# Sixteen low-half products of the first attention are made by GpSimd in place of VectorE

## The chip, the cores and the metric

The kernel runs on one core of one Trainium2 chip. The metric is the device time of one execution in microseconds (us), from the first to the last instruction and the little around them. Before the change three runs took 1171.39, 1173.42 and 1175.44 us; their median is 1173.42 us.

The core has five instruction queues. PE (TensorE) multiplies matrices, ACT (ScalarE) applies functions and scales, DVE (VectorE) and POOL (GpSimd) do elementwise work, SP (SyncE) starts transfers. Each queue is worked off in the order in which its instructions stand, and queues wait for each other by semaphores.

## The reference

The program is a two-layer encoder on 512 tokens of width 1024, in float32. Layer 0 is the even one. Its attention has two groups of eight heads that share one output projection. Group A is grouped-query attention with rotary positions. Group B (the diff's word for it is kind B) is latent attention, in which 32 of the 96 query and key columns carry the rotary part:

```
h = x
for layer in range(DEPTH):
    hn = rmsnorm(h, norm_mix[layer])
    if layer % 2 == 0:   h = h + hybrid_attention(hn, ...)      # A heads, B heads, concatenate, @ w_out
    else:                h = h + neighbourhood_attention(hn, ...)
    h = h + sq_relu_mlp(rmsnorm(h, norm_ffn[layer]), ...)

rope_1d: [x1*cos - x2*sin, x2*cos + x1*sin]
hybrid:  mixed = concatenate([oa, ob]);  return mixed @ w_out
```

The change touches the hybrid attention of layer 0 alone, which in the profile lies between about 68 and 264 us.

## The kernel before

**Two halves of a number.** The products must keep nearly float32 precision on a multiplier that takes rounded numbers. Every operand is therefore split: a high half, which ACT writes by a copy into the rounded type, and a low half, the number minus its high half, which costs one two-input subtraction on DVE or POOL. A product is three matmuls: high by high, high by low, low by high (`mm3`, lines 545, 546 and 547). `split` (line 899) makes the two halves of an activation: ACT at line 906, the low half at line 903. `chunk` (lines 206 to 250) makes those of weights: the high half at line 236, or at 246 where heads are regrouped, the low half at line 226. A weight chunk that is given an engine uses that engine for its low half; without one it is DVE's.

**The attention.** `attend` (line 1036) goes through the 16 heads, four blocks of 128 queries each. For each block PE makes the scores (line 1070, tile `s`), DVE scales them and takes the minimum (line 1074), ACT makes the exponentials (line 1076), DVE the reciprocal of the sum (line 1077), POOL scales by it (line 1078, in the tile `shared`). Some blocks later PE transposes the result (line 1045, tile `t`), ACT and DVE split it (lines 1047 and 1048), and PE multiplies with the values (line 1058, tile `o`). There are five score buffers in `shared`, two banks for `s`, two for `t`, one for `o`, three `mm` for the work in between.

**The work in between.** While heads run, PE is also given the projections of the B heads (`projB`, whose rotary part goes through `rope`), and, from the 36th block on, the output projection of the first four head pairs (`out_proj`). `fold` adds the halves of a finished head (line 1022) and, after the second head of a pair, splits the pair; the pairs are the operands of the output projection. The last four pairs are projected after the last head.

**Rotary positions.** `rope` makes a shuffled copy on DVE (line 603), a product with the cosines on POOL (line 605), a product with the sines on DVE (line 606) and the sum on DVE (line 609). In group A the shuffles of later tiles are transfers (`far`), the sine product is POOL's, and the sum is made at line 674 and split at lines 676 and 677.

**What sets the order.** In this part of the program a scheduler places the instructions on PE, ACT, DVE and POOL at build time, from its own estimates of what each costs. A change of engine for one instruction therefore reorders others. On the chip each queue keeps that order. POOL's queue also starts the transfers of line 832, which add sums of later weights in memory.

Of the kernel before, what the change touches and what calls it, by code (L numbers as in the profile page):

```python
# [12 lines left out]
ALU = mybir.AluOpType  # L13
# [5 lines left out]
P = 128  # L19
# [16 lines left out]
def encoder_kernel(ctx: ExitStack, tc: tile.TileContext, ins, out, dbg=None):  # L36
# [555 lines left out]
    sw16 = [q ^ 16 for q in range(32)]  # L592
    sw8 = [q ^ 8 for q in range(32)]

    def rope(src, cos, sin, mask, n=P, far=False):

        sh = scratch()
        if far:
            q = mask[0]
            for b in range(0, n, q):  # L600
                SP.dma_start(sh[b : b + q, :], src[b ^ q : (b ^ q) + q, :])
        else:
            DVE.stream_shuffle(sh[0:n, :], src[0:n, :], mask)
        c = scratch()
        POOL.tensor_tensor(c[0:n, :], src[0:n, :], cos[0:n, :], op=ALU.mult)
        (POOL if far else DVE).tensor_tensor(sh[0:n, :], sh[0:n, :], sin[0:n, :], op=ALU.mult)
        if far:
            return c, sh
        DVE.tensor_tensor(c[0:n, :], c[0:n, :], sh[0:n, :], op=ALU.add)
        return c  # L610
# [287 lines left out]

    w_uq, w_ukv = ins["ev_b_w_uq"][0], ins["ev_b_w_ukv"][0]

    def split(src, dst, then=lambda: None):
        def low():
            DVE.tensor_tensor(dst[:, 1, :], src, f32(dst[:, 0, :]), op=ALU.subtract)  # L903
            then()

        ACT.activation(dst[:, 0, :], src, AF.Copy)
        soon(low)
# [3 lines left out]
    def projB(g, last):  # L911
# [5 lines left out]
        def q_part():  # L917
            CQ = [s_.pair() for s_ in cqS]
            banks = three(3)
            for m in (2, 0, 1):  # L920
                for k in range(3):
                    hi, lo = (z[:, k % 2, m * P : (m + 1) * P] for z in weights(iq[k // 2]))
                    mm3(banks[m], hi, lo, CQ[k][:, 0, :], CQ[k][:, 1, :], k == 0, k == 2)
                    yield MM3
                if m == 2:
                    qc = scratch()
                    ACT.activation(qc, banks[2], AF.Copy)
                    qr = rope(qc, cosB, sinB, sw8)
                    stg = Slot()
                    split(qr, stg.pair())  # L930
                else:

                    Q.extend(Slot() for _ in range(2))
                    qa, qb = Q[2 * m].pair(), Q[2 * m + 1].pair()
                    split(banks[m], qa)
                    SP.dma_start(f32(qb[0:64, :, :]), f32(qa[64:128, :, :]))
                    for e, q in enumerate((qa, qb)):
                        j = 2 * m + e
                        SP.dma_start(f32(q[64:96, :, :]), f32(stg.pair()[32 * j : 32 * j + 32, :, :]))
            stg.free()  # L940
            if last:
                for s_ in cqS:
                    s_.free()
# [53 lines left out]

    w_out = ins["ev_w_out"][0]

    def out_proj(w, k0, ok, cols, name):  # L1000

        def ev(j, b):
            m = cols[j]
            DVE.tensor_tensor(hT[:, m, :], hT[:, m, :], b, op=ALU.add)
        gen = product(w, k0, ok, [(P * m, P) for m in cols], ev, three if name else None)
        if name:
            return name, gen
        for _ in gen:
            pass
# [4 lines left out]
    def fold(o, e):  # L1014
# [6 lines left out]
        def add():  # L1021
            DVE.tensor_tensor(pair[a : a + 64, :], o[0:64, :], c[0:64, :], op=ALU.add)
            if e:
                O.append(Slot())
                soon_a(lambda o=O[-1]: split(pair, o.pair()))

        soon(add)

# [122 lines left out]
    def step(h, i):  # L1151
        n = count[0]
        count[0] += 1
        if n == 35:

            ok = [s_.pair() for s_ in O]
            assert len(ok) == 4
            fill.add(*out_proj(w_out, 0, ok, [0, 1, 2], "out"))
            projB(1, True)
            fill.add(*out_proj(w_out, 0, ok, [3, 4, 5], "out"))  # L1160
            fill.add(*out_proj(w_out, 0, ok, [6, 7], "out"))
        if n == 22:
            beat.update(every=4.2, work=ahead0.steps())
        fill.run(1.5)
# [841 lines left out]
```

## Time and profile before

| what | value |
|---|---|
| median of three runs | 1173.42 us |
| the profiled execution's own time | 1173.18 us |
| its span, first to last instruction | 1171.4 us |
| PE busy over the span | 1144.9 us, 98% |
| DVE busy | 919.4 us, 78% |
| ACT busy | 668.2 us, 57% |
| POOL busy | 463.6 us, 40% |
| granted TensorE clock | 0.998 |

About 1.8 us of the profiled execution lie outside its span. The profiler takes one execution, and the times of single instructions are from it. A row of the timeline gives the start in us, the duration in us, the engine, the line, the operation, output and inputs, and in brackets the idle time ahead of it with what ended it. Matmuls overlap: one of 512 columns is shown with about 0.39 us, while the next starts 0.23 us later, so that a wait on PE is read from the distance of the starts rather than from the busy time.

### The profile page before, as it was taken

Reading aid. Unit: us, or ns where it says so; the run is one execution under the profiler, and the core shown is the slowest. Engines: PE = TensorE matmul, PEld = TensorE weight load, DVE = VectorE, ACT = ScalarE, POOL = GpSimd, SP = SyncE. Lnnn points to the kernel's source line nnn. Section 1 sums busy time; section 2 is a strip of 40 time slices with the busy share of each in tenths; the row PEclk is TensorE's granted clock in tenths of the full one; section 3 lists DMA queues with packets and bytes.
Section 4 is the critical chain, followed back from the end, with each engine's and each line's share of the span. In section 5 each row is a group of like instructions: output and inputs, shape, how many; then the busy total and the mean of one; then the engine's idle time right before and its main releaser. Section 6 shows DMA issues by size and latency. Waiting matters only on the chain.

```text
span 1171.4 us, 20855 instructions
## 1 busy us (share of the span) xinstructions
PE 1144.9 (98%) x7596; PEld 1029.6 (88%) x7596; DVE 919.4 (78%) x1617; ACT 668.2 (57%) x1147; POOL 463.6 (40%) x486
## 2 busy tenths in 40 slices
PE   9989999999999999999999999999999999999996
PEld 8667778888799999999988998988788999999995
DVE  5788988778978787998474676767896878799845
ACT  5468576664536656756253555645552665675625
POOL 3267253333668795000002243333185898600000
PEclk9999999999999999999999999999999999999999
DMA  7123467664577666768426497778566666765702
GB/s 273 55 79 84 122 147 202 176 143 129 114 172 196 162 149 198 234 215 278 131 82 163 131 247 190 191 189 209 178 128 183 170 166 158 193 208 174 249 2 72
DMA packets 129543, 191.55 MB, mean 164 GB/s; under 512 B 12659, under 2 KB 81184, under 8 KB 128736
## 3 DMA queue, kind: packets, MB, share of 16 engines
q1 hardware_dynamic: 112304, 136.61, 37.1%
q0 software_dynamic: 14976, 29.38, 15.5%
q10 hardware_dynamic: 2160, 24.22, 6.2%
q8 instruction: 60, 0.98, 0.4%
q14 instruction: 43, 0.35, 0.1%
HBM read 167.75 MB, written 52.43 MB: 188 GB/s over the span
## 4 chain that ended last, share of the span: by engine, by line
PE 79%; DVE 10%; DMA 4%; ACT 3%; issue 2%; POOL 1%; SPq 0%; DVEq 0%; POOLq 0%; ACTq 0%
PE mm L547 7%; PE mm L545 7%; PE mm L546 7%; PE t L1444 3%; PE t L1443 2%; PE t L1445 2%; PE mm L418 2%; PE mm L416 2%; PE mm L417 2%; PE s L1070 2%; PE o L1058 2%; PE mm L1445 2%; PE mm L1443 2%; PE mm L1444 2%; PE t L1045 2%
## 5 line engine op out<-in xcount | busy, mean ns | idle before, releaser
L545 PE MATMUL mm<-a,whi 128*128 128x512 f32 x407 | 164.8, 407 | 0.3 <-ACT whi L236 0.2
L547 PE MATMUL mm<-a,wlo 128*128 128x512 f32 x407 | 160.2, 395 | 1.6 <-DVE wlo L226 1.5
L546 PE MATMUL mm<-a,whi 128*128 128x512 f32 x407 | 160.9, 395 | 0.1
L337 DVE TENSOR_TENSOR wlo<-raw,whi 128x896 fp32r<-128x896 f32 x80 | 110.5, 1388 | 28.6 <-ACT whi L336 28.4
L236 ACT ACTIVATE whi<-raw 128x1024 fp32r<-128x1024 f32 (+3 forms) x86 | 80.4, 939 | 86.4 <-PE s L546 29.7
L226 DVE TENSOR_TENSOR wlo<-raw,whi 128x1024 fp32r<-128x1024 f32 (+4 forms) x83 | 99.2, 1197 | 36.1 <-ACT whi L236 34.4
L336 ACT ACTIVATE whi<-raw 128x896 fp32r<-128x896 f32 x80 | 75.4, 949 | 83.6 <-PE o L546 22.9
L547 PEld LDWEIGHTS mm<-a,wlo 128*128 128x128 f32 x407 | 76.4, 188 | 19.4 <-DVE wlo L226 3.0
L545 PEld LDWEIGHTS mm<-a,whi 128*128 128x128 f32 x407 | 76.5, 188 | 16.1 <-ACT whi L236 1.3
L546 PEld LDWEIGHTS mm<-a,whi 128*128 128x128 f32 x407 | 76.8, 189 | 14.1 <-DVE a L903 0.4
L1609 POOL DMA_DIRECT2D a<-a x16 | 8.7, 545 | 185.7 <-PE mm L546 169.2
L1078 POOL TENSOR_SCALAR shared<-shared,ti 128x512 f32<-128x512 f32 x64 | 48.3, 758 | 84.5 <-DVE ti L1077 53.5
L418 PE MATMUL mm<-a,wlo 128*128 128x256 f32 x280 | 78.8, 282 | 0.7 <-DVE wlo L337 0.7
L417 PE MATMUL mm<-a,whi 128*128 128x256 f32 x280 | 78.5, 280 | 0.0
L416 PE MATMUL mm<-a,whi 128*128 128x256 f32 x280 | 78.4, 280 | 0.0
L1444 PE MATMUL t<-a,whi 128*128 128x256 f32 x264 | 74.2, 281 | 0.6 <-DVE a L1389 0.5
L1443 PE MATMUL t<-a,whi 128*128 128x256 f32 x264 | 73.9, 280 | 0.0
L1445 PE MATMUL t<-a,wlo 128*128 128x256 f32 x264 | 73.9, 280 | 0.0
L1701 POOL TENSOR_SCALAR shared<-shared,ti 128x256 f32<-128x256 f32 x64 | 35.5, 566 | 95.9 <-DVE ti L1700 83.6
L330 POOL TENSOR_TENSOR raw<-raw 128x512 f32<-128x512 f32 x40 | 67.8, 1695 | 3.1
L1341 DVE TENSOR_TENSOR wlo<-a,whi 128x1024 fp32r<-128x1024 f32 x42 | 51.1, 1221 | 19.4 <-ACT whi L1340 19.4
L329 POOL TENSOR_TENSOR raw<-raw 128x256 f32<-128x256 f32 x40 | 45.1, 1127 | 44.0 <-DMA raw<-in_ffn_w_up_dram 26.1
(399 smaller groups left out, 4007.3 us busy)
## 6 DMA issues: line engine op xcount, KB each, us to landing
made<-in_ffn_w_down_dram ACTq DMA_DIRECT2D x44, 512.0 KB
raw<-in_ffn_w_up_dram SPq DMA_DIRECT2D x80, 256.0 KB
a<-made SPq DMA_DIRECT2D x70, 256.0 KB
made<-in_ffn_w_down_dram POOLq DMA_DIRECT2D x44, 256.0 KB, 6.1
made<-made POOLq DMA_DIRECT2D x44, 256.0 KB, 6.8
raw<-in_ffn_w_down_dram SPq DMA_DIRECT2D x36, 256.0 KB
raw<-in_ffn_w_down_dram SPq DMA_DIRECT2D x16, 512.0 KB
raw<-in_od_w_qkv_dram SPq DMA_DIRECT2D x64, 128.0 KB
```

Of the source, the lines that this page charges most:

```text
L226: z = lambda: (eng or DVE).tensor_tensor(to, src, f32(high), op=ALU.subtract)
L236: ACT.activation(hi[:, 0:m], raw[:, 0:m], AF.Copy)
L337: DVE.tensor_tensor(lo[:, 0:896], raw[:, 128:1024], f32(hi[:, 0:896]), op=ALU.subtract)
L416: PE.matmul(o, wh, x[:, 0], start=kp == 0 and n in (0, 1, 3, 5), stop=False, skip_group_check=True)
L417: PE.matmul(o, wh, x[:, 1], start=False, stop=False, skip_group_check=True)
L418: PE.matmul(o, wl, x[:, 0], start=False, stop=kp == self.np - 1, skip_group_check=True)
L545: PE.matmul(o, wh, xh, start=first, stop=False)
L546: PE.matmul(o, wh, xl, start=False, stop=False)
L547: PE.matmul(o, wl, xh, start=False, stop=last)
L1443: PE.matmul(o, wh, x[:, 0], start=first and m % 2 == 0, stop=False, skip_group_check=True)
L1444: PE.matmul(o, wh, x[:, 1], start=False, stop=False, skip_group_check=True)
L1445: PE.matmul(o, wl, x[:, 0], start=False, stop=last, skip_group_check=True)
```

## The change

Four kinds of elementwise products go from DVE's queue to POOL's; what is computed stays the same.

- The sine product of `rope` for the B queries (line 606), once for each of the two groups of four heads: 2 instructions of 128x512.
- The low halves of finished head pairs (line 903), 8 instructions of 128x512.
- The low halves of the output projection's weights for the first four pairs (line 226): two chunks each for the columns 0 to 2, 3 to 5 and 6 to 7, that is 4 instructions of 128x768 and 2 of 128x512.

The pieces for the last four pairs' weights stay on DVE, and so do the sine product of the rotary key and the low halves of Q and K. In the second layer's attention, whose order is held by hand (`fixed`), the pairs' low halves stay on DVE too.

```diff
-    def rope(src, cos, sin, mask, n=P, far=False):
+    def rope(src, cos, sin, mask, n=P, far=False, pool=False):
...
-        (POOL if far else DVE).tensor_tensor(sh[0:n, :], sh[0:n, :], sin[0:n, :], op=ALU.mult)
+        (POOL if far or pool else DVE).tensor_tensor(sh[0:n, :], sh[0:n, :], sin[0:n, :], op=ALU.mult)
...
-    def split(src, dst, then=lambda: None):
+    def split(src, dst, then=lambda: None, eng=None):
         def low():
-            DVE.tensor_tensor(dst[:, 1, :], src, f32(dst[:, 0, :]), op=ALU.subtract)
+            (eng or DVE).tensor_tensor(dst[:, 1, :], src, f32(dst[:, 0, :]), op=ALU.subtract)
...
-                    qr = rope(qc, cosB, sinB, sw8)
+                    qr = rope(qc, cosB, sinB, sw8, pool=True)
...
-    def out_proj(w, k0, ok, cols, name):
+    def out_proj(w, k0, ok, cols, name, eng=None):
...
-        gen = product(w, k0, ok, [(P * m, P) for m in cols], ev, three if name else None)
+        gen = product(w, k0, ok, [(P * m, P) for m in cols], ev, three if name else None, eng=eng)
...
-                soon_a(lambda o=O[-1]: split(pair, o.pair()))
+                soon_a(lambda o=O[-1]: split(pair, o.pair(), eng=None if fixed[0] else POOL))
...
-            fill.add(*out_proj(w_out, 0, ok, [0, 1, 2], "out"))
+            fill.add(*out_proj(w_out, 0, ok, [0, 1, 2], "out", POOL))
             projB(1, True)
-            fill.add(*out_proj(w_out, 0, ok, [3, 4, 5], "out"))
-            fill.add(*out_proj(w_out, 0, ok, [6, 7], "out"))
+            fill.add(*out_proj(w_out, 0, ok, [3, 4, 5], "out", POOL))
+            fill.add(*out_proj(w_out, 0, ok, [6, 7], "out", POOL))
```

In the next rows `a_982` is the first finished pair, `sc_852` the sine product of a group A rotation, whose sum (line 674) DVE makes, `wlo_1034` a weight's low half, and `ti_1016` the sums of a block of scores. A plus marks what stands there now, a minus what stood there before. POOL's queue at the first pair, some 95 us into the span:

```order
 L226 TENSOR_TENSOR wlo_1034<-raw_695,whi_1033 128x512
 L606 TENSOR_TENSOR sc_852<-sc_852,a_129 128x512
+L903 TENSOR_TENSOR a_982<-sc_841,a_982 128x512
 L1078 TENSOR_SCALAR shared<-shared,ti_1016 128x512
 L1078 TENSOR_SCALAR shared<-shared,ti_1043 128x512
```

The pair's low half now stands directly behind the sine product, and ahead of the scaling of two blocks of scores.

POOL's queue where the output projection's weights are first prepared, some 154 us into the span (`ti_1705` and `ti_1720` are the sums of two blocks of scores):

```order
 L1078 TENSOR_SCALAR shared<-shared,ti_1669 128x512
 L1078 TENSOR_SCALAR shared<-shared,ti_1705 128x512
+L226 TENSOR_TENSOR wlo_1852<-raw_1031,whi_1851 128x768
+L226 TENSOR_TENSOR wlo_1856<-raw_1843,whi_1855 128x768
 L1078 TENSOR_SCALAR shared<-shared,ti_1720 128x512
 L832 DMA made_614<-in_ffn_w_down_dram 128x512
```

Two weight halves now stand ahead of the scaling with `ti_1720`, the result of which PE transposes as `t_1774`. PE's queue at the same place (`mm_1839` to `mm_1841` are the banks of the output projection, `o_1683` a head's output):

```order
+L1058 MATMUL o_1683<-a_1674,a_128 128x256
 L1045 MATMUL t_1727<-cst,shared 128x128 x4
-L1058 MATMUL o_1683<-a_1674,a_128 128x256
-L545 MATMUL mm_1839<-a_982,whi_1851 128x512
-L546 MATMUL mm_1839<-a_982,whi_1851 128x512
-L545 MATMUL mm_1840<-a_982,whi_1851 128x512
-L546 MATMUL mm_1840<-a_982,whi_1851 128x512
-L545 MATMUL mm_1841<-a_982,whi_1851 128x512
-L546 MATMUL mm_1841<-a_982,whi_1851 128x512
 L1058 MATMUL o_1683<-a_1675,a_128 128x256
 L1058 MATMUL o_1683<-a_1674,a_128 128x256
```

Six matmuls of the output projection that stood ahead of `o_1683`'s second part, and so ahead of `t_1774`, now stand behind it.

PE's queue at the end of the attention (`a_2680` and `a_2817` are the last two pairs, and `L546` reads a pair's low half):

```order
-L547 MATMUL mm_2822<-a_2680,wlo_2832 128x512
-L545 MATMUL s_2823<-a_2680,whi_2831 128x512
-L546 MATMUL s_2823<-a_2680,whi_2831 128x512
-L547 MATMUL s_2823<-a_2680,wlo_2832 128x512
 L545 MATMUL mm_2820<-a_2817,whi_2831 128x512
 L545 MATMUL mm_2821<-a_2817,whi_2831 128x512
-L545 MATMUL mm_2822<-a_2817,whi_2831 128x512
 L546 MATMUL mm_2820<-a_2817,whi_2831 128x512
 L547 MATMUL mm_2820<-a_2817,wlo_2832 128x512
```

Four matmuls of the pair before that stood ahead of the last pair's first ones, and one of the last pair's own, have moved behind its low half's first use.

## The prediction

> **What bounds the kernel now.** I read the page first, then the busy times by stretch of the first attention, then PE's waits there, and last the timeline at the places of the edits.
>
> ```profile
> span 1171.4 us, 20855 instructions
> PE 1144.9 (98%) x7596; PEld 1029.6 (88%) x7596; DVE 919.4 (78%) x1617; ACT 668.2 (57%) x1147; POOL 463.6 (40%) x486
> ```
>
> PE is busy for 98% of the span, and the change takes nothing from PE. It can gain only where PE stands idle, and it loses where PE is made to wait. The next rows give length and busy time of PE, weight loads, DVE, ACT and POOL by stretch:
>
> ```profile
> 85.00:110.00 25.00, 24.09 (x147) 20.02 (x146) 20.70 (x51) 21.11 (x48) 18.76 (x22) 1.00 0.30 77
> 110.00:129.00 19.00, 17.86 (x93) 11.98 (x91) 16.78 (x47) 10.86 (x24) 10.83 (x10) 1.00 0.25 66
> 129.00:153.00 24.00, 22.36 (x142) 18.45 (x140) 22.88 (x52) 19.25 (x43) 7.01 (x9) 1.00 0.66 177
> 153.00:165.00 12.00, 12.00 (x77) 10.54 (x77) 11.22 (x29) 10.51 (x23) 8.19 (x10) 1.00 0.60 177
> 165.00:186.00 21.00, 19.93 (x114) 16.83 (x113) 16.74 (x36) 11.57 (x26) 10.70 (x13) 1.00 0.54 140
> 186.00:260.00 74.00, 73.83 (x418) 61.09 (x418) 60.05 (x130) 49.63 (x101) 26.46 (x34) 1.00 0.71 179
> ```
>
> DVE is the full engine only from 129 to 165 us (34.1 of 36 us); POOL is fullest from 85 to 110 and from 153 to 165. From 186 us on PE has 0.17 us of idle time in 74, so nothing moved there can gain. In the same window (85 to 260 us) PE's own waits were ended by:
>
> ```profile
> PE o L1058 <- DVE a L1048: 2.3, 3, 1.1
> PE t L574 <- DVE rsB L625: 0.6, 1, 0.6
> PE s L1070 <- DVE ti L1074: 0.6, 1, 0.6
> PE t L1045 <- DVE a L1048: 0.4, 1, 0.4
> PE t L1045 <- DVE ti L1077: 0.3, 1, 0.3
> ```
>
> These five sum to 4.2 us, all ended by DVE. That is about the most a faster DVE can return.
>
> **The change part by part.** What is moved costs this on either engine (busy us, mean ns of one):
>
> ```profile
> L903 DVE TENSOR_TENSOR a<-sc,a 128x512 fp32r<-128x512 f32 x16 | 12.5, 785 | 1.3 <-ACT a L906 1.3
> L606 DVE TENSOR_TENSOR sc<-sc,a 128x512 f32<-128x512 f32 x3 | 3.8, 1272 | 0.0
> L226 DVE TENSOR_TENSOR wlo<-raw,whi 128x768 fp32r<-128x768 f32 x5 | 5.7, 1139 | 0.0
> L226 DVE TENSOR_TENSOR wlo<-raw,whi 128x512 fp32r<-128x512 f32 x2 | 1.4, 684 | 0.5 <-ACT whi L236 0.5
> L606 POOL TENSOR_TENSOR sc<-sc,a 128x512 f32<-128x512 f32 x3 | 4.3, 1441 | 0.0
> L226 POOL TENSOR_TENSOR wlo<-raw,whi 128x512 fp32r<-128x512 f32 x10 | 13.8, 1384 | 4.4 <-ACT whi L246 3.2 <-ACT whi L236 1.1
> L226 POOL TENSOR_TENSOR wlo<-raw,whi 128x128 fp32r<-128x128 f32 x2 | 0.9, 462 | 0.0
> ```
>
> DVE loses 8 x 0.785 + 2 x 1.27 + 4 x 1.14 + 2 x 0.68 = 14.7 us of work. POOL gets 12 instructions of 512 columns and 4 of 768. An undisturbed one of 512 takes 1.3 us (1.29 and 1.31 in the rows quoted below). No row has 768 columns on POOL. From 128 to 512 the time rises by 0.83 us, or 2.2 ns a column, so I estimate 1.3 + 256 x 0.0022 = 1.85 us. POOL thus gains 12 x 1.3 + 4 x 1.85 = 23 us. Each product gets later by 0.6 to 0.7 us where both engines are free, and on POOL the scaling of scores queues behind it.
>
> A second cost is that the two engines shut each other out:
>
> ```profile
> 95.58 0.92 DVE L903 TENSOR_TENSOR a<-sc,a 128x512 fp32r<-128x512 f32 x1
> 95.89 1.75 POOL L606 TENSOR_TENSOR sc<-sc,a 128x512 f32<-128x512 f32 x1
> 97.68 0.69 DVE L674 TENSOR_TENSOR sc<-sc,sc 128x512 f32<-128x512 f32 x1 [1.19 <-POOL sc L606]
> 99.16 0.50 PE L1070 MATMUL s<-a,a 128*128 128x512 f32 x1 [0.56 <-DVE ti L1074]
> 180.25 0.90 POOL L1078 TENSOR_SCALAR shared<-shared,ti 128x512 f32<-128x512 f32 x1
> 180.81 2.15 DVE L606 TENSOR_TENSOR sc<-sc,a 128x512 f32<-128x512 f32 x1
> 180.91 1.48 POOL L605 TENSOR_TENSOR sc<-sc,a 128x512 f32<-128x512 f32 x1
> ```
>
> At 95.89 POOL's sine product took 1.75 us instead of 1.3, beside DVE's subtraction. At 180.81 a DVE product of 0.68 us waited until two POOL instructions that followed each other had ended (182.39), and ended at 182.96. So DVE does not get in between two POOL instructions that stand ready. [...]
>
> *Pair 0, around 97 us.* POOL's sine product would end at 97.2 instead of 97.65, since DVE's subtraction is gone. But the pair's low half follows without a wait and holds POOL until 98.5. DVE's sum L674 waits for the sine product, finds POOL running again, and ends at 99.1 instead of 98.37. L1074 behind it is what PE's scores at 99.16 waited for. So +0.8 us. If DVE won the race it would be 0.45 sooner: bounds -0.4 and +0.9.
>
> *Pair 1, around 117 us.*
>
> ```profile
> 116.85 0.93 DVE L903 TENSOR_TENSOR a<-sc,a 128x512 fp32r<-128x512 f32 x1 [0.44 <-ACT a L906]
> 117.70 0.68 DVE L674 TENSOR_TENSOR sc<-sc,sc 128x512 f32<-128x512 f32 x1
> 119.08 0.69 DVE L677 TENSOR_TENSOR sc<-sc,a 128x512 fp32r<-128x512 f32 x1
> ```
>
> The low half stood ahead of the sum L674 with 0.93 us; without it DVE is that much sooner. But on POOL it now stands directly between two scalings, and L677, with both inputs in SBUF, can be shut out by 0.7 + 1.3 + 0.7 = 2.7 us, which leaves it 1.8 us later than before. Behind it comes the rotary key, at whose end L574 waited 0.6 us for DVE. Bounds -0.9 and +1.8; I take +0.7, a little over the middle, since POOL's instructions stand back to back here too.
>
> *The first sine product of kind B and the weights, 135 to 160 us.*
>
> ```profile
> 135.45 0.74 DVE L603 STREAM_SHUFFLE sc<-sc 128x512 f32<-128x512 f32 x1
> 135.81 1.31 POOL L605 TENSOR_TENSOR sc<-sc,a 128x512 f32<-128x512 f32 x1
> 136.68 0.98 DVE L606 TENSOR_TENSOR sc<-sc,a 128x512 f32<-128x512 f32 x1
> 138.25 0.89 DVE L609 TENSOR_TENSOR sc<-sc,sc 128x512 f32<-128x512 f32 x1
> 153.81 0.70 POOL L1078 TENSOR_SCALAR shared<-shared,ti 128x512 f32<-128x512 f32 x1 [3.18 <-DVE ti L1077]
> 155.55 0.69 POOL L1078 TENSOR_SCALAR shared<-shared,ti 128x512 f32<-128x512 f32 x1 [1.04 <-DVE ti L1077]
> 158.21 1.29 POOL L226 TENSOR_TENSOR wlo<-raw,whi 128x512 fp32r<-128x512 f32 x1
> ```
>
> The sine product has to follow the cosine product on POOL: 137.1 + 1.3 = 138.4. In DVE's new order only one instruction stands between the shuffle and L609, so DVE stands still from about 136.7 to 138.4. Of the 0.98 us that leave DVE nothing is gained there. What is gained is the third pair's low half later on, which took DVE 0.92 us as pair 0's did. Both together can bring DVE ahead by at most 1.9 us. Then, at 154, two weight halves of 1.85 us stand on POOL between two scalings that lay 1.74 us apart: now 0.7 + 3.7 = 4.4, that is 2.65 us later for `t_1774`, less the up to 1.9 by which DVE is ahead: 0.75 to 2.65. Six matmuls that covered PE (6 x 0.23 = 1.4 us) now stand behind it, so the upper end is 4.05. I take the middle, +2.4. Below, if POOL begins the halves early and keeps up, PE's idle 1.64 us of 129 to 153 us come back: -1.6.
>
> *The second sine product, 181 us.* DVE took 2.15 us for it, mostly shut out. On POOL it ends at 182.2 + 1.3 = 183.5, and L609 behind it starts where it did (183.55): 0, bounds -0.3 and +0.3.
>
> *The other weight halves and pairs, 186 to 250 us.* POOL has 26.5 of 74 us of work and PE no idle time: 0, at worst +0.5 where a scaling queues behind a weight half. If that cover were gone, each would cost its 0.6 us.
>
> *The last pair, 253 us.*
>
> ```profile
> 253.22 0.69 DVE L903 TENSOR_TENSOR a<-sc,a 128x512 fp32r<-128x512 f32 x1 [0.70 <-ACT a L906]
> 253.24 0.97 PE L545 MATMUL mm<-a,whi 128*128 128x512 f32 x3
> 254.05 0.41 PE L546 MATMUL mm<-a,whi 128*128 128x512 f32 x1
> ```
>
> The low half was ready at 253.91 and PE used it at 254.05 without a wait. On POOL it is ready at 253.2 + 1.3 = 254.5. In the new order PE comes to it earlier by three matmuls net (five less ahead of it, two more that come from further up), at about 253.3, or 253.7 after the wait for ACT's high half. It has nothing else until 254.5: 0.4 + 0.8 = +1.2. If the halves come sooner or PE later, nothing: bounds 0 and +1.7.
>
> The sum is 0.8 + 0.7 + 2.4 + 0 + 0 + 1.2 = **+5.1 us** on the profiled execution's own 1173.18 us (span 1171.4 and 1.8 around it): **1178.3 us**. That execution is 0.24 us below the median of the runs, well within their 4 us, so I give the same number for the median.
>
> **The rivals.** *DVE is what counts (faster).* The place is 129 to 153 us, where DVE is busy for 22.88 of 24 us and PE idle for 1.64. If POOL ends the sine product before DVE needs it, that is if DVE stands still less than the 1.9 us taken from it, then the waits on DVE shrink, with all five of the list gone by 4.2 us: 1169.0. For it speaks that all five end on DVE; against it, that at 97, 117 and 181 us DVE then waits for POOL.
>
> *Nothing moves (same).* POOL is idle for 60% of the span, the small delays fall behind other matmuls, and gains and losses of under 1 us each cancel: 1173.2. For it speaks that PE loses only 0.17 us after 186 us, however late POOL is; against it, that cover was taken away at two places. [...]
>
> *POOL becomes the bound at every place (much slower).* With the upper ends at pairs 0 and 1, the weights and the end it is 0.9 + 1.8 + 4.05 + 1.7 = 8.5 us: 1181.6. For it speaks that POOL has 8.19 of 12 us already from 153 to 165 and gets 3.7 more; against it, that DVE's 14.7 us must be worth something.
>
> **How the numbers follow.** The forecast gets 0.40, much slower 0.10, nothing moves 0.30, DVE counts 0.20. About 0.3%, or 3.5 us, can be told from no change: slower 0.50, same 0.30, faster 0.20. All good ends together give -0.4 - 0.9 - 1.6 - 0.3 = -3.2 us; with the faster rival at 1169.0, and a tenth left out on each side, the range is 1169.5 to 1182 us. The forecast's own range is 1175.5 to 1181.
>
> **What would show it.** Right: L674 near 97 us starts behind a POOL L903 and ends after 99; DVE idle ahead of L609 by over 1 us near 137, with POOL L606 named; two POOL L226 of about 1.85 us directly ahead of a L1078, and PE idle ahead of the transposes after it; PE waiting for POOL's L903 at the end of the attention. Wrong: PE's idle time from 85 to 186 us below the 4.8 us of now, or POOL's L226 of 768 columns in under 1.4 us, or DVE's L674 at once behind L606.

## The result, and the profile after

The changed kernel takes **1179.85 us** (median of 8 runs, 1176.63 to 1182.07). The kernel before, timed beside it, takes 1174.27 us (median of 8 runs, 1171.39 to 1176.56). The ratio is **1.0046, with a 95% interval of 1.0031 to 1.0061**: slower by some 5.4 us. The profiled execution took 1182.07 us, with a span of 1180.3; it is the slowest of the eight, and 1.5 us of that are accounted for below.

The same stretches as before, with length and busy time of PE, weight loads, DVE, ACT and POOL, then the granted clock:

```profile
85.00:110.00 25.00, 23.09 (x138) 18.54 (x138) 21.13 (x50) 20.16 (x46) 19.62 (x22) 1.00 0.30 79
129.00:153.00 24.00, 21.95 (x136) 18.23 (x134) 18.98 (x51) 14.94 (x33) 6.98 (x9) 1.00 0.56 151
153.00:165.00 12.00, 9.47 (x55) 8.44 (x56) 10.68 (x25) 10.54 (x25) 10.21 (x11) 0.86 0.60 138
186.00:260.00 74.00, 72.17 (x424) 60.81 (x423) 54.42 (x125) 48.72 (x101) 38.04 (x43) 1.00 0.68 175
```

From 129 us on DVE has become lighter (18.98 of 24 us from 129 to 153 us, where it had 22.88; from 85 to 110 us it is level, 21.13 against 20.70), and PE nevertheless stands idle more: 1.91, 2.05 and 2.53 us in the first three rows, against 0.91, 1.64 and 0.00. Of the 1.83 us in the last row (0.17 before), 1.26 are one wait at 193.06 us that the kernel before has too, at 184.89 us and so outside its row. The granted clock of 0.86 from 153 to 165 us is new.

PE's largest waits from 85 to 270 us (total in us, number, longest):

```profile
PE o L1058 <- DVE a L1048: 2.7, 3, 1.3
PE t L1045 <- DVE ti L1077: 2.1, 2, 1.5
PE s L1070 <- DVE ti L1074: 1.2, 1, 1.2
PE mm L546 <- POOL a L903: 1.1, 1, 1.1
PE o L1058 <- ACT a L1047: 0.9, 1, 0.9
PE t L574 <- DVE rsB L625: 0.7, 1, 0.7
```

One of them ends on POOL. The others still end on DVE and ACT, although DVE was relieved of 14.7 us. The reciprocal L1077 in the second row is only the name that the profile found last. A transpose, by its rows, reads `cst` and `shared`, and both times PE begins 0.15 us behind the end of an eviction L1048, the subtraction that empties a bank of transposes: 102.66 + 0.68 = 103.34 and PE at 103.48, 156.62 + 0.68 = 157.30 and PE at 157.45. Where the profile names the eviction, the distance is the same (154.95 + 0.67 = 155.62 and PE at 155.77, in a row below). So these are waits for evictions too.

What POOL's new work costs, from the groups by form (busy us, mean ns of one):

```profile
L903 POOL TENSOR_TENSOR a<-sc,a 128x512 fp32r<-128x512 f32 x8 | 11.8, 1469 | 11.1 <-ACT a L906 11.1
L226 POOL TENSOR_TENSOR wlo<-raw,whi 128x768 fp32r<-128x768 f32 x4 | 7.4, 1839 | 0.9 <-ACT whi L236 0.9
```

The estimate of 1.85 us for 768 columns was right (1.839). A pair's low half takes 1.47 us on average: five of the eight took 1.29 or 1.30, three 1.71 (at 121.62 us), 1.82 (222.68) and 1.77 (260.49), the first and the last of these beside a DVE instruction that had begun before them.

The timeline at the first pair:

```profile
98.25 1.29 POOL L606 TENSOR_TENSOR sc<-sc,a 128x512 f32<-128x512 f32 x1
99.49 1.29 POOL L903 TENSOR_TENSOR a<-sc,a 128x512 fp32r<-128x512 f32 x1
99.57 1.76 DVE L674 TENSOR_TENSOR sc<-sc,sc 128x512 f32<-128x512 f32 x1 [1.56 <-POOL sc L606]
101.33 0.73 DVE L1074 CUSTOM_DVE_ANT_0 shared<-s,zeros,scA 128x512 f32<-128x512 f32 x1
102.11 0.73 PE L1070 MATMUL s<-a,a 128*128 128x512 f32 x2 [1.17 <-DVE ti L1074]
```

DVE's sum L674 found POOL on the low half, 0.08 us after that had begun, and took 1.76 us where it had taken 0.69.

The timeline from 141 to 163 us:

```profile
141.20 0.69 DVE L609 TENSOR_TENSOR sc<-sc,sc 128x512 f32<-128x512 f32 x1 [1.51 <-POOL sc L606]
153.35 1.29 POOL L903 TENSOR_TENSOR a<-sc,a 128x512 fp32r<-128x512 f32 x1
153.42 1.76 DVE L903 TENSOR_TENSOR a<-sc,a 128x512 fp32r<-128x512 f32 x1
155.18 0.73 DVE L1074 CUSTOM_DVE_ANT_0 shared<-s,zeros,scA 128x512 f32<-128x512 f32 x1
155.84 0.87 DVE L988 SCALAR_TENSOR_TENSOR a<-mm,rsB,a 128x256 fp32r<-128x256 f32 x2
156.62 0.68 DVE L1048 TENSOR_TENSOR a<-t,a 128x512 fp32r<-128x512 f32 x1
157.45 1.09 PE L1045 MATMUL t<-cst,shared 128*128 128x128 f32 x4 [1.48 <-DVE ti L1077]
158.19 3.67 POOL L226 TENSOR_TENSOR wlo<-raw,whi 128x768 fp32r<-128x768 f32 x2
162.35 0.69 POOL L1078 TENSOR_SCALAR shared<-shared,ti 128x512 f32<-128x512 f32 x1 [0.48 <-DVE ti L1077]
```

Two things are to be seen. The weights' halves (158.19) end at 161.86, and the scaling behind them starts at 162.35 because DVE's reciprocal is late, not because POOL was: the forecast's largest term stands where it was said to stand, and PE does not wait for that scaling. The first mark of the weights is a wait of 0.30 us for POOL's scaling at 165.88 us, behind the next weight half. And PE's long wait at 157.45 lies before the weights. DVE's eviction L1048 at 156.62 (it empties the bank of the transposes `t_1676`) stands behind a L1074 and two L988 there. In the kernel before it stood ahead of them.

The timeline at the last pair:

```profile
260.49 1.77 POOL L903 TENSOR_TENSOR a<-sc,a 128x512 fp32r<-128x512 f32 x1 [8.18 <-ACT a L906]
262.31 0.50 PE L546 MATMUL mm<-a,whi 128*128 128x512 f32 x1 [1.12 <-POOL a L903]
```

Where the time went, by matching the matmuls of both traces (by how much later the same amount of PE's work is begun): 0.8 us at the start and 1.5 at 75 us, both outside the change; +1.2 at the first pair; +0.3 to 0.5 at the second; about +4.1 from 138 to 165; +0.2 at 183; +1.3 at the last pair. That is 9.5 us in this one execution, while the medians differ by 5.6.

Two of these contain the granted clock. The same view by stretches of 3.41 us:

```profile
71.74:75.15 3.41, 1.06 (x6) 0.53 (x4) 2.99 (x14) 1.96 (x3) 0.00 (x0) 1.00 0.65 242
75.16:78.57 3.41, 3.41 (x10) 2.63 (x9) 2.19 (x8) 2.53 (x8) 0.69 (x1) 0.50 0.00 0
153.67:157.08 3.41, 1.41 (x10) 0.97 (x9) 3.41 (x7) 2.99 (x9) 2.57 (x3) 1.00 0.43 55
157.08:160.49 3.41, 3.04 (x13) 2.98 (x14) 2.63 (x7) 2.56 (x5) 2.94 (x3) 0.50 0.65 142
```

After each of two stretches in which PE was busy for only 1.06 and 1.41 of 3.41 us, it ran for 3.413 us at half the clock (0.50 in the rows). The first of them costs about 1.5 us: from the start of L1070 at 74.57 us to that of L1045 at 79.71 PE takes 5.14 us, where it took 3.61 for the same matmuls in the kernel before (73.75 to 77.36). The one at 75 us lies ahead of the change, at a wait that the kernel before has too; so 1.5 us of this execution is chance. The one at 157 us follows the waits above and is part of the 4.1.

### The profile page after: what moved, and what is told of

The parts are those of the page before. It is cut to its first block, busy times and chain, and to the rows that moved or that the text cites. A ratio compares the mean times of both kernels' runs of the same rounds, so it can differ in the third digit from the quotient of the medians.

```text
span 1180.3 us, 20859 instructions
## 1 busy us (share of the span) xinstructions
PE 1148.9 (97%) x7596; PEld 1033.2 (88%) x7596; DVE 911.3 (77%) x1601; ACT 668.5 (57%) x1147; POOL 481.0 (41%) x502
## 4 chain that ended last, share of the span: by engine, by line
PE 74%; DVE 13%; DMA 4%; ACT 3%; issue 3%; POOL 2%; SPq 0%; DVEq 0%; ACTq 0%; POOLq 0%
PE mm L547 7%; PE mm L546 6%; PE mm L545 6%; DVE wlo L337 2%; PE t L1444 2%; PE t L1443 2%; PE t L1445 2%; PE s L1070 2%; PE mm L418 2%; PE mm L416 2%; PE mm L417 2%; PE o L1058 2%; PE mm L1445 2%; PE mm L1443 2%; PE mm L1444 2%
## 5 line engine op out<-in xcount | busy, mean ns | idle before, releaser
L546 PE MATMUL mm<-a,whi 128*128 128x512 f32 x407 | 161.5, 397 | 1.2 <-POOL a L903 1.1
L226 DVE TENSOR_TENSOR wlo<-raw,whi 128x1024 fp32r<-128x1024 f32 (+4 forms) x77 | 93.6, 1218 | 34.4 <-ACT whi L236 32.8
L546 PEld LDWEIGHTS mm<-a,whi 128*128 128x128 f32 x407 | 76.9, 189 | 15.7 <-POOL a L903 1.6
L330 POOL TENSOR_TENSOR raw<-raw 128x512 f32<-128x512 f32 x40 | 64.4, 1611 | 3.1
```

Source lines behind the costliest of these rows:

```text
L226: z = lambda: (eng or DVE).tensor_tensor(to, src, f32(high), op=ALU.subtract)
L546: PE.matmul(o, wh, xl, start=False, stop=False)
```

## The experiments

Each kernel was timed beside the kernel before, with 7 to 12 runs (`o_before` 5, `o_dve` 4). In one table (median in us; kernel before on the same chip; ratio with its 95% interval):

| kernel | median | before | ratio |
|---|---|---|---|
| e1_pairs: pairs' low halves alone | 1178.28 | 1174.44 | 1.0040 (1.0029 to 1.0051) |
| e2_weights: weights' low halves alone | 1174.27 | 1174.44 | 0.9999 (0.9988 to 1.0009) |
| e3_sine: sine products alone | 1177.72 | 1174.44 | 1.0028 (1.0016 to 1.0039) |
| e4_last_back: all but the last pair | 1178.88 | 1174.44 | 1.0042 (1.0029 to 1.0056) |
| o_after: new engines, old order | 1176.26 | 1173.66 | 1.0024 (1.0013 to 1.0036) |
| o_before: old engines, new order | 1178.71 | 1173.66 | 1.0047 (1.0035 to 1.0060) |
| o_sine: sine products alone, old order | 1173.43 | 1173.66 | 0.9994 (0.9983 to 1.0005) |
| c_evict_first: evictions earlier | 1173.88 | 1173.66 | 1.0005 (0.9994 to 1.0016) |
| o_dve: DVE's and ACT's new order alone | 1182.63 | 1173.52 | 1.0080 (1.0064 to 1.0095) |
| o_late: one eviction later | 1176.44 | 1173.52 | 1.0028 (1.0017 to 1.0040) |
| o_best: five instructions earlier | 1175.15 | 1173.52 | 1.0016 (1.0008 to 1.0025) |
| o_tuned: three places mended | 1172.29 | 1172.96 | 1.0003 (0.9989 to 1.0017) |

### The three parts alone, and the change without the last pair

Only the pairs (the parameter of `split` as in the change):

```diff
-                soon_a(lambda o=O[-1]: split(pair, o.pair()))
+                soon_a(lambda o=O[-1]: split(pair, o.pair(), eng=None if fixed[0] else POOL))
```

> Only the low halves of the finished head pairs go to GpSimd; sine products and the output projection's weights stay on VectorE. Theory A (the pairs' low halves carry most of the loss: pair 0 +1.2 us, pair 1 +0.4, the third pair about +1.0 through VectorE's L903 that it shuts out, the last pair +1.4, as the changed kernel's trace shows them): about 4.0 us above the kernel before. Theory B (the terms of the prediction: 0.8 + 0.7 + 1.2 for pairs 0, 1 and the last, nothing for the third): 2.7 us above it. Theory C (nothing but the new order of the matmuls and half-clock stretches of about 1.6 us each count): 0 to 1.6 us above it, and no wait of PE for GpSimd's L903 at the end of the attention.

Only the weights:

```diff
-            fill.add(*out_proj(w_out, 0, ok, [0, 1, 2], "out"))
+            fill.add(*out_proj(w_out, 0, ok, [0, 1, 2], "out", POOL))
...
```

> Only the low halves of the output projection's first half of weights go to GpSimd. Theory A (GpSimd has room for them; one set of transposes waits about 0.45 us, and VectorE gets 6 us of work less): between -0.5 and +0.5 us of the kernel before. Theory B (the prediction's largest term: two halves of 1.85 us stand ahead of a scaling, and the transposes behind it come 0.75 to 2.65 us late): 1 to 2.7 us above the kernel before, with PE idle by over 1 us ahead of a set of transposes that waits for GpSimd's L1078 between 154 and 165 us.

Only the sine products:

```diff
-                    qr = rope(qc, cosB, sinB, sw8)
+                    qr = rope(qc, cosB, sinB, sw8, pool=True)
```

> Only the two sine products of the second kind go to GpSimd. Theory A (VectorE stands still for about 1.5 us ahead of L609 near 137 us and gains 0.98 us for it; the third pair's low half is still VectorE's): 0.3 to 1 us above the kernel before, all of it between 136 and 160 us, and 0.2 at the second product near 181 us. Theory B (as in the prediction: what VectorE loses there is made up, the price lies in the weights): within 0.3 us of the kernel before. Theory C (VectorE is the bound from 129 to 165 us, so each instruction taken from it is a gain): 0.5 to 1 us below it.

The changed kernel with the eighth pair back on DVE:

```diff
-                soon_a(lambda o=O[-1]: split(pair, o.pair(), eng=None if fixed[0] else POOL))
+                soon_a(lambda o=O[-1], n=len(O): split(pair, o.pair(), eng=POOL if n != 8 and not fixed[0] else None))
```

> The changed kernel, with the low half of the last head pair back on VectorE. Theory A and the prediction agree on the place: PE's wait of 1.1 us for GpSimd's L903 at the end of the attention goes, and the time falls by 1.2 to 1.4 us against the changed kernel, to about 4 us above the kernel before. Theory C (the wait is only moved: behind the projection PE meets the next wait at the same time as before): no change against the changed kernel, 5.4 us above the kernel before.

Measured by the medians: pairs +3.8 us, weights -0.2, sine products +3.3, all but the last pair +4.4. Theory B falls with the weights, which cost nothing that these runs can tell. Their largest mark in the trace is one wait of PE (list of PE's waits, e2_weights):

```profile
PE mm L547 <- POOL wlo L226: 0.7, 1, 0.7
```

Theory A is right on the pairs and the weights and wrong on the sine products, which cost three times what it allowed. Theory C names the order for the pairs, but with a bound of 1.6 us that is too low, and for the sine products a gain that isn't there. The three parts give 3.8 - 0.2 + 3.3 = 6.9 us, more than the 5.4 of the whole change. The intervals of the three (each about 1.2 us to either side) are too wide for this sum alone to show that the prices don't add up; the next experiments settle that. With the last pair back on DVE, PE's wait of 1.1 us at the end of the attention is gone from the trace and with it the lag of 1.3 us there; the times (1.0042 against 1.0046) can't tell it.

What the sine products alone did is to be seen in their timeline near 155 us (e3_sine), above the same place in the kernel before:

```profile
153.50 0.73 DVE L1074 CUSTOM_DVE_ANT_0 shared<-s,zeros,scA 128x512 f32<-128x512 f32 x1
154.16 0.87 DVE L988 SCALAR_TENSOR_TENSOR a<-mm,rsB,a 128x256 fp32r<-128x256 f32 x2
154.95 0.67 DVE L1048 TENSOR_TENSOR a<-t,a 128x512 fp32r<-128x512 f32 x1
155.77 0.63 PE L1045 MATMUL t<-cst,shared 128*128 128x128 f32 x4 [0.82 <-DVE a L1048]
```

```profile
149.68 0.67 DVE L1048 TENSOR_TENSOR a<-t,a 128x512 fp32r<-128x512 f32 x1
150.27 0.86 DVE L988 SCALAR_TENSOR_TENSOR a<-mm,rsB,a 128x256 fp32r<-128x256 f32 x2
150.49 0.63 PE L1045 MATMUL t<-cst,shared 128*128 128x128 f32 x4 [0.45 <-DVE a L1048]
151.05 0.74 DVE L1074 CUSTOM_DVE_ANT_0 shared<-s,zeros,scA 128x512 f32<-128x512 f32 x1
```

None of these instructions has changed its engine. It is the order that differs: before, the eviction of `t_1676`, then two L988 and L1074; now L1074 and the two L988 first. The scheduler places instructions by its own estimate of when each can start, so an instruction with a new engine moves its neighbours. That gave a new theory, O: a good part of the loss is the new order, not the new engines.

### Engines and order apart

To test it, the order was held. Each instruction between the first and the last that the change moves (873 on PE, 211 on ACT, 230 on DVE, by the order of the kernel before) gets an edge (`NoSync`) to its neighbour on the same engine, which fixes the order; what these edges cost on the chip was not timed by itself, but `o_sine`, which has them, took 0.9994 of the time of the kernel before:

```diff
+def hold_order(tc):
+    info = mybir.DependencyInfo(mybir.DependencyClass.NoSync, mybir.DependencyReason.DATA)
+    for names in ORDER.values():
+        for x, y in zip(names, names[1:]):
+            tc.add_manual_dep(tc.nc.get_inst_by_name(f"I-{y}"), f"I-{x}", info, reason="order held")
```

With `ORDER` from the kernel before (less what left DVE) in the changed kernel:

> The changed kernel with the order of the kernel before on TensorE, ScalarE and VectorE through the first attention; only the 16 moved instructions leave VectorE's row, and GpSimd takes them where its own order puts them. Theory O (a good part of the loss is the new order: VectorE's eviction of the transposes t_1676 stands behind the next block's L1074 and two L988 then, which makes PE late by 1 to 2 us between 150 and 158 us): the loss falls from 5.4 us to 2.5 to 3.5 us above the kernel before; what stays is pair 0's 1.2 us, pair 1's 0.4, VectorE standing still ahead of L609, and a part of the last pair's 1.4. Theory E (the engines alone make the loss, order is nothing): 5.4 us above the kernel before, as the changed kernel.

With `ORDER` from the changed kernel in the kernel before:

> The other corner: every operation on the engine of the kernel before, in the order that the changed kernel has on TensorE, ScalarE and VectorE through the first attention (the 16 instructions stand on VectorE where its scheduler puts them between the others). Theory O: 1.5 to 3 us above the kernel before, lost between 150 and 158 us, with PE waiting ahead of t_1727 for VectorE's L1048. Theory E: within 0.5 us of the kernel before.

And the sine products alone in the order of the kernel before:

> Only the two sine products on GpSimd, in the order of the kernel before on TensorE, ScalarE and VectorE. The same move in its own order was 3.3 us slower. Theory O: 0.5 to 1.2 us above the kernel before (VectorE stands still for 1.5 us ahead of L609 and is spared 0.98 us; the eviction of t_1676 keeps its place). Theory E: 3 us above it, as in its own order.

The four corners, as ratios to the kernel before:

| | old order | new order |
|---|---|---|
| old engines | 1 | 1.0047 (1.0035 to 1.0060) |
| new engines | 1.0024 (1.0013 to 1.0036) | 1.0046 (1.0031 to 1.0061) |

Theory E falls. Theory O holds for the first run, but is too low for the new order on the old engines (1.5 to 3 us expected, 5.0 measured) and too high for the sine products (0.5 to 1.2 expected, -0.2 measured). The new order costs as much as the whole change with every operation on its old engine. The engines alone cost half of it, and nothing that these runs can tell once the order is new. The equal totals are in part luck, for they are not made up alike. By the lag of its trace, `o_before` loses 0.6 us at the first pair, 1.0 at the second, 2.7 from 147 to 165, and 1.6 net from 190 to 250, where the changed kernel loses nothing net; it doesn't have the 1.3 of the last pair. That the delays of the engines fall into time in which PE waits anyway would explain the corner, but is not shown. The sine products cost nothing measurable in the old order; their 3.3 us came with the new one.

PE's waits with the old engines in the new order (o_before):

```profile
PE o L1058 <- DVE a L1048: 3.8, 5, 1.5
PE o L1058 <- ACT a L1047: 1.9, 3, 0.8
PE t L1045 <- DVE ti L1077: 1.9, 3, 0.7
```

These are the waits of the changed kernel without POOL's and the shut-out: evictions of transposes on DVE (L1048) and on ACT (L1047), late in their rows. The third row is evictions as well: all three times PE begins 0.15 us behind the end of an L1048. In the kernel before these rows had 2.3, 0 and 0.3 us.

With the new engines in the old order (o_after), the first two of these are what POOL does to its neighbours, and the third is the last pair:

```profile
PE s L1070 <- DVE ti L1074: 1.2, 1, 1.2
PE t L574 <- DVE rsB L625: 1.0, 1, 1.0
PE mm L546 <- POOL a L903: 0.4, 1, 0.4
```

And the first sine product in the old order (o_sine):

```profile
138.40 1.18 DVE L609 TENSOR_TENSOR sc<-sc,sc 128x512 f32<-128x512 f32 x1 [0.59 <-POOL sc L606]
```

DVE stands still for 0.59 us here, not 1.5, because in the old order another eviction stands ahead of L609. L609 then takes 1.18 us beside POOL's scaling, which began 0.05 us before it (138.35), where it took 0.69 in the changed kernel (141.20). By the lag PE is 0.4 us later there, and that is lost among the rest.

### Which row, and one instruction

The old engines, with DVE and ACT in the new order and PE in the old (`ORDER` mixed from both):

> Every operation on the engine of the kernel before; ScalarE and VectorE in the order of the changed kernel, TensorE in the order of the kernel before (but for a few matmuls behind 250 us). With TensorE in the new order as well this was 5.0 us slower than the kernel before. Theory V (the rows of VectorE and ScalarE carry the price: evictions of transposes stand behind longer work): 3.5 to 5 us above the kernel before. Theory P (TensorE's row carries it: matmuls that covered its waits stand elsewhere): 0 to 1.5 us above it.

It is 9.1 us slower, beyond both theories. PE waits 5.0 us in one piece there (o_dve):

```profile
157.88 0.69 DVE L1048 TENSOR_TENSOR a<-t,a 128x512 fp32r<-128x512 f32 x1 [2.41 <-issue]
158.71 1.09 PE L1045 MATMUL t<-cst,shared 128*128 128x128 f32 x4 [5.01 <-DVE ti L1077]
```

Here too PE begins 0.14 us behind an eviction (157.88 + 0.69 = 158.57), and ahead of this eviction DVE itself stood still for 2.41 us for something that the profile doesn't name. Neither kernel has a wait of that length at this place. So DVE's and ACT's new rows are enough to lose time, but since the mix of old and new rows makes a wait of its own, this run doesn't show how much of the change's loss is theirs. PE's new row with the other two in the old order was not run.

One instruction alone, in the otherwise unchanged order of the kernel before:

```diff
 L988 SCALAR_TENSOR_TENSOR a_1625<-mm_1624,rsB,a_1625 128x4x64
 L1077 RECIPROCAL ti_1669<-ti_1669 128x1
-L1048 TENSOR_TENSOR a_1675<-t_1676,a_1674 128x4x128
 L988 SCALAR_TENSOR_TENSOR a_1625<-mm_1624,rsB,a_1625 128x4x64
 L988 SCALAR_TENSOR_TENSOR a_1658<-mm_1657,rsB,a_1658 128x4x64
 L1074 ISA shared,ti_1705<-s_1702,zeros,scA 128x512
 L1074 ISA ti_1705 128x1
+L1048 TENSOR_TENSOR a_1675<-t_1676,a_1674 128x4x128
```

> The kernel before in its own order, with one instruction moved: VectorE's eviction L1048 of the transposes t_1676 stands behind two L988 and the next block's L1074, where the changed kernel and the two part changes with GpSimd's low halves or sine products have it, 1.6 us of VectorE's work later. If that one place makes the loss between 150 and 158 us: 1 to 1.6 us above the kernel before, with PE waiting that long for this L1048. If PE's other work covers it there: within 0.4 us of the kernel before, and the loss needs the other moves too.

It costs 2.9 us (1.0028, 1.0017 to 1.0040), above both expectations. Its timeline (o_late):

```profile
152.20 0.88 DVE L988 SCALAR_TENSOR_TENSOR a<-mm,rsB,a 128x256 fp32r<-128x256 f32 x2 [0.47 <-ACT a L987]
152.99 0.74 DVE L1074 CUSTOM_DVE_ANT_0 shared<-s,zeros,scA 128x512 f32<-128x512 f32 x1
153.66 0.69 DVE L1048 TENSOR_TENSOR a<-t,a 128x512 fp32r<-128x512 f32 x1
154.50 0.63 PE L1045 MATMUL t<-cst,shared 128*128 128x128 f32 x4 [2.48 <-DVE a L1048]
```

PE waits 2.48 us for the bank, where it had waited 0.45: 2.0 us, more than the 1.6 us of work that was put ahead, because the L988 now in front wait 0.47 us for ACT. In this trace a stretch at half clock follows (0.50 from 155.73 to 159.14 us), another 0.9. So the place of this one eviction in DVE's row is enough for a loss of that size between 150 and 158 us.

### Versions for the other side

If the place of the evictions counts, putting them earlier should gain. First by a rule, all on the old engines:

```diff
-            DVE.tensor_tensor(l3, t3, f32(h3), op=ALU.subtract)
+            with tc.high_priority(offset=60 if not fixed[0] else 0): DVE.tensor_tensor(l3, t3, f32(h3), op=ALU.subtract)
```

> A version for the other side: the kernel before, all on VectorE, but its scheduler is told to place VectorE's evictions of the transposes (L1048) ahead of what was written up to 60 instructions earlier, which takes them ahead of reciprocals, of low halves and of a L988. Theory O (the place of the evictions in VectorE's row is what counts; PE's waits for L1048 are 2.7 of its 4.2 us of waits for VectorE): 0.5 to 2.5 us below the kernel before. Theory E: within 0.5 us of it.

No change (1.0005), so theory O falls here. Then by hand, at the waits of the kernel before (four instructions on DVE and one on ACT moved in the held order; two of them):

```diff
 L603 STREAM_SHUFFLE sc_2074<-sc_2072 128x512
+L1048 TENSOR_TENSOR a_2047<-t_2095,a_2046 128x4x128
 L606 TENSOR_TENSOR sc_2074<-sc_2074,a_130 128x512
...
 L1022 TENSOR_TENSOR sc_1455<-o_1522,sc_1606 64x512
+L1048 TENSOR_TENSOR a_1590<-t_1640,a_1589 128x4x128
 L903 TENSOR_TENSOR a_1617<-sc_1615,a_1617 128x512
 L1077 RECIPROCAL ti_1635<-ti_1635 128x1
-L1048 TENSOR_TENSOR a_1590<-t_1640,a_1589 128x4x128
```

> The kernel before, all on its engines, with four instructions moved on VectorE and one on ScalarE, each at a wait that the trace of the kernel before shows: L1074 of ti_1043 ahead of L674 (VectorE stands still there for 1.19 us, and PE then waits 0.56 us for this L1074), the eviction of t_1640 ahead of a low half on both engines (PE waits 0.76 us for it), L861 behind the rotary key's chain (0.64 us in the chain for which L574 waits 0.6 us), and the eviction of t_2095 ahead of the second sine product, which stands shut out by GpSimd (PE waits 1.07 us for it). Theory O (a wait is made or taken away by the place in the row): 1.5 to 2.9 us below the kernel before. If the next wait comes up in each place: within 0.7 us of it.

It is slower by 0.16% (1.0008 to 1.0025), against both expectations. Some waits were taken away, and others came up. Behind the place near 147 us, where the eviction of `t_1640` was put ahead of a low half and of the reciprocal of `ti_1635`, PE gained 0.4 us, and then waited longer than it had (o_best):

```profile
152.76 0.69 DVE L1048 TENSOR_TENSOR a<-t,a 128x512 fp32r<-128x512 f32 x1 [0.95 <-DMA a<-a]
153.59 0.63 PE L1045 MATMUL t<-cst,shared 128*128 128x128 f32 x4 [1.93 <-POOL shared L1078]
```

PE's row names POOL's scaling, but that is the scaling of the next block: in the kernel before, the same transposes began at 150.49 us, before this scaling had ended (149.93 + 0.69 = 150.62 there). What freed PE is the eviction of `t_1676`, which ended 0.14 us before PE began, and DVE had stood still for 0.95 us ahead of it until a transfer was done. Why the transfer was late was not followed. At 181 us PE gained 1.3 us, and lost them again before 198, since DVE's next L1074 came no sooner; near 208 us it lost another 2.0, most of it in a wait of 1.68 us for DVE's L988. A last version moves at each place what hangs on the moved instruction too (near 147 us the two reciprocals and an exponential; near 97 us three instructions into DVE's and ACT's idle time; the transfers' order held as well):

> The kernel before on its own engines, its order held (the DMA queue's too), and three places mended with what hung on each: near 97 us VectorE uses its 1.19 us of standing still ahead of L674 for the eviction of t_1050 and L1074 of ti_1043, and ScalarE evicts t_1080 ahead of L676 (PE's waits of 0.56 and 0.29 us there); near 147 us the eviction of t_1640 stands ahead of the low half on both engines, and this time the exponential and the reciprocals of ti_1635 and ti_1669, on which GpSimd's scalings and the next transposes wait, stand ahead as well (PE's waits of 0.76, 0.6 and 0.48 us); near 181 us the eviction of t_2095 stands ahead of the sine product that GpSimd shuts out (1.07 us; the earlier trial gained 1.3 us there). Theory O: 1.5 to 3 us below the kernel before. If the next wait comes up in each place again: between 1 us below it and 1 us above it.

It is level with the kernel before (1.0003, 0.9989 to 1.0017). In its trace 1.2 us are gained near 101 us and given back by 105, and 1.3 are gained at 184 us, of which 1.15 are given back by 194. No version here beats the kernel before.

## Why the prediction was right, and where its reasons were wrong

The forecast was 1178.3 us in a range of 1169.5 to 1182; measured were 1179.85, slower, as the likeliest case said. That the sum of 5.1 us comes so near to the measured 5.4 is in part luck: its largest term has the wrong cause and is little more than half of what was lost there, and by the lag of the trace the places of the change sum to 7.2 us in the profiled execution. PE's idle time from 85 to 186 us rose from 4.8 to 7.5 us, so the direction came by waits of PE, as was said, though most of them are for evictions and not for POOL.

**Pair 0 (+0.8).** The steps came as told: L674 starts behind a POOL L903 (99.49) and ends at 101.33, PE's L1070 waits 1.17 us. The size was 1.2. In the four corners 0.6 of it is there with the new engines in the old order and 0.6 with the old engines in the new order, where ACT's row differs (an exponential ahead of an eviction). The forecast had only the first.

**Pair 1 (+0.7).** 0.3 to 0.5, within the bounds. The shut-out went the other way: DVE's L677 (121.39, 0.81 us) began before POOL's low half (121.62), which took 1.71 us, and L574 waited 0.7 instead of 0.6 us. With the new engines in the old order that wait is 1.0 us.

**The first sine product and the weights (+2.4).** This is the step that failed. That DVE stands still ahead of L609 was right (1.51 us, POOL's L606 named), and so was the price of a weight half (1.839 us). But the weights cost nothing alone (0.9999), the scaling behind them waited for DVE, and PE did not stand idle ahead of the transposes of its result, as the prediction had it. The prediction, like the part on the change, also gave the wrong transposes: they run three blocks behind the scores, so that the result of `ti_1720` is `t_1799`, not `t_1774`. In the place of the queue on POOL stands the order: the eviction of `t_1676` behind two L988 and L1074 (2.9 us by itself), and the third pair's low half on POOL, beside which DVE's L903 took 1.76 us at 153.42. About 4.1 us were lost here, of which at most 1.5 are the half clock (half of the 3.04 us that PE was busy in it); the kernel with all but the last pair, which kept its clock here (1.00), lost 3.5. The order carries most of that: the sine products alone, where this eviction stands just as late, lost 2.9 us here, and the new order on the old engines 2.7. How much the low half adds was not timed by itself.

**The second sine product (0).** 0.2. **The other weights and pairs (0).** Right: nothing net; 0.8 us lost near 213 us are back by 253.

**The last pair (+1.2).** PE waited 1.12 us for POOL's L903, and lagged by 1.3; with the pair back on DVE that wait was gone. The low half took 1.77 us, not the 1.3 of the forecast, since DVE's L226 had begun before it; the size came out by luck in so far. In the old order, with its cover, the wait is 0.4.

**The rivals.** That DVE counts was wrong: DVE lost 14.7 us of work and PE's waits for it did not shrink. The reading behind it, that a wait of PE for DVE is worth its length, is not borne out by the last three versions either: where such waits were taken away, others came up at the next place. That POOL becomes the bound everywhere was wrong too; it ends one of PE's larger waits. That nothing moves fell as well, though the weights, the second sine product and, in the old order, the first one are places where it held.

What no step priced was the order. The prediction counted moved matmuls as lost cover, and, but for the look at DVE's row ahead of L609, let that row stand as it was without the instructions that left it. In the old order the change costs 2.6 us by the medians. By the lag of its trace, which is one execution, 0.6, 0.4 and 0.6 us lie at the first, the second and the last pair, where the forecast had 0.8, 0.7 and 1.2, 0.4 behind the first sine product, and 0.8 each near 155 and 205 us, where PE waits for the transfer of an operand and for DVE's L988, for which it had no term.

## What to carry to other kernels

Where a scheduler sets the order at build time, an instruction on another engine is two changes: hold the order and time each by itself before explaining either. In a pipeline in which PE is busy for 98%, look for what frees its banks: one eviction of 0.67 us put behind 1.6 us of other work cost 2.9 us, and 14.7 us of work taken from the same engine gained nothing. And a wait that is taken away is not yet a gain: here what was gained was given back within 15 us, also in the version that moved along what hung on the moved instructions.

## What of the hardware was not expected

In these profiles PE's clock fell to one half after a stretch of much idle time, be it one wait or several. In the changed kernel the two stretches at half clock inside the kernel last 3.413 us each (from 75.16 and 157.08 us), and they lie on one grid of 3.413 us with the one at the end of the span (from 1174.25 us): 24 and 322 steps behind the first. In `o_dve` one lasts twice that (157.12 to 163.94 us, 0.50 in both steps). Eight steps of such a grid at full clock had PE idle for 1.97 us or more (busy for 1.44 or less, ends of matmuls being modelled), and all eight were followed by half clock: at 71.74 and 153.67 us in the changed kernel, at 150.98 with the pairs alone, at 70.40 and 152.32 in `o_late`, at 71.79 and 153.71 in `o_dve`, at 71.92 in `o_tuned`. Of the steps at full clock with 1.90 us or less, from 40 to 290 us in the kernel before and in the changed kernel, none was. The nearest on both sides, from the pairs alone and from the kernel before:

```profile
150.98:154.39 3.41, 1.44 (x10) 0.92 (x8) 3.41 (x9) 2.98 (x7) 2.10 (x4) 1.00 0.48 44
154.39:157.80 3.41, 3.41 (x14) 3.11 (x14) 3.19 (x8) 2.82 (x7) 0.92 (x2) 0.50 0.62 148
```

```profile
69.86:73.27 3.41, 1.51 (x7) 0.92 (x5) 2.99 (x10) 2.40 (x3) 0.58 (x1) 1.00 0.79 259
73.27:76.68 3.41, 2.93 (x13) 2.28 (x14) 3.23 (x11) 2.47 (x7) 0.13 (x1) 1.00 0.03 10
```

So the same wait of 2.4 us near 73 us cost 1.5 us more in the changed kernel and nothing in the kernel before, by where it fell on the grid: from 72.22 to 74.57 us it lay within one step in the changed kernel (71.74 to 75.15), and from 71.37 to 73.75 across the border at 73.27 in the kernel before. The changed kernel without the last pair had PE idle for 2.35 us from 153 to 165 us, nearly as much as the changed kernel (2.53), but spread over two steps (1.92 us busy from 150.66 us, 2.36 from 154.07), and kept its clock (1.00 in both). Gaps of 0.88 and 1.48 us close to each other were enough in the changed kernel (ahead of 155.58 and 157.45 us). That this chance is a part of the 3 to 8 us by which runs of one kernel differ fits the numbers, but was not shown, since only one run of each kernel has a trace.

In the changed kernel DVE and POOL shut each other out in both directions: a POOL low half of 1.29 us took 1.71 (121.62 us) and 1.77 (260.49) beside a DVE instruction that had begun before it, and a DVE instruction of 0.69 took 1.76 (99.57 and 153.42) beside a POOL low half that had begun before it. DVE's evictions L1048, which read a bank of transposes, took 0.66 to 0.69 us in all 64 instances of the kernel before and of the changed kernel, also beside a POOL low half (0.68 at 122.12 us).
